# One v projection earlier in the hand-written order, held inverses, and elementwise work moved from GpSimd to VectorE and from VectorE to ScalarE

## The chip, the cores and the metric

One core of one Trainium2 chip runs the whole program. The metric is device microseconds (us) of one execution. An execution under the hardware profiler gives the trace that is read below; the other executions are timed without it.

## What is computed

The reference is one residual block over 2048 tokens of width 1024, in float32, with two causal token mixers side by side:

```
h = x @ w_in                          # split into q, k, v, z, b, a | q, k, v, z | gate_a, gate_b
A: q, k, v = silu(short causal conv of width 4); q, k normalized
   beta = sigmoid(b); g = -exp(a_log) * softplus(a + dt_bias)
   gated delta rule over 4 heads of 128: in a chunk a triangular system is inverted, a state S runs across chunks
   y_a = rmsnorm(o) * w * silu(z)
B: attention over a window of 128 tokens, 8 query heads, 2 key heads of 64, rotary on 16 of 64,
   a sink logit in the softmax's denominator; y_b = attention * silu(z)
merged = sigmoid(gate_a) * (y_a @ w_a) + sigmoid(gate_b) * (y_b @ w_b)
out = layernorm(2**0.25 * x + merged @ w_out) * ln_g + ln_b
```

## The kernel before, in words

The 2048 tokens go in four chunks of 512 (`NCH`). Every large product is made of three matmuls of a reduced-precision type (`prods`, L175 to L177): each operand is split into a high half and a low half (the rounding rest), and high x high, high x low and low x high are summed in PSUM. So a weight piece of 128 x 512 needs a copy that rounds (ScalarE, L156) and a subtraction that leaves the rest (GpSimd, L157). `split` does this the first time a piece is met, and stores both halves to DRAM (`keep`, L141); later chunks load the halves (L152). Most pieces are met in chunk 0, the output projection's at the start of chunk 1. Four buffers (`W_SPLIT`) hold pieces on their way.

**Order on TensorE.** It is written by hand. `ORDER` is a list of words, one per projection: `kv` (keys and values of B with b and a), `k0 q0 v0` (one head's k, q, v of A), `z0`, `w0` (a pair of query groups of B with their z), `g` (a gate), `p` (a quarter of the output projection of the chunk before). Chunk 0 has its own list, `ORDER_FIRST`. These dense pieces are cut into steps, and between steps the class `Order` puts the steps of side tasks: it counts planned nanoseconds, and a side task's next step is written when its due time (`LAT_...`) has passed. `finish` writes a task's steps out at once where something needs its end. TensorE executes in exactly the written order; on the other engines and on the DMA queue of SyncE (SP) a scheduler orders the instructions when the program is built, and each engine then executes its own list in order.

**The side tasks of a head of A.** `front` (L352) makes k's and q's statistics and products; the 32 x 32 diagonal blocks go through DRAM (L400, L402) into the tile `su`. `inverse` (L423) is spawned `LAT_M` = 4400 planned ns later and inverts them on VectorE: `small_inverse` (L918) begins with a memset into `su` (L924) that is pinned to its place in the written order, then pairs of a product and a reduction (L936, L937), sixteen of each, written at a pace of 420 + 40n ns. `levels` (L428) joins the blocks on TensorE; `back` (L475) transposes v (L485), scales it (`vt`, L491), and runs four blocks of a chain in which TensorE and VectorE take turns (L497, `bt` L499, L502, `wc` L504, L508, S L509). It ends with `osum`, an rsqrt and `dt` (L522), and `delta_gate` (L525) follows. `back` of head 0 waits for v0.

**`conv_silu` (L309)** serves q, k and v: ScalarE moves PSUM into `xs` (L313), VectorE copies three halo columns in (L314) and out (L319), one scaled copy on ScalarE (L316), three multiply-adds (L318), a tanh, a product (L321). One buffer `xs` serves all.

**`attend` (L574)**, spawned by `window_q`, goes over 4 blocks of tokens for each of two groups, 32 blocks in all. Per block: scores for two key heads v (L591, L592), then for each v on its own: two masked maxima (L599), `nm`, `es`, exponentials with a sum on ScalarE (L605, L608), sum plus sink, times 2, reciprocal, and the product with the 128 x 512 tile on VectorE (L614). `LAT_SM` = 9200 planned ns later TensorE transposes the first half's probabilities (L622), then the second's, and multiplies by the values (L630).

`project` (L674) and `layer_norm` (L703) finish the chunk before, at the start of the next one: four pieces `p`, then normalization on VectorE, which reads gamma and beta from DRAM (L716).

Of the kernel before, what the change touches and what calls it, by code (L numbers as in the profile page):

```python
# [8 lines left out]
F32 = mybir.dt.float32  # L9
F32R = mybir.dt.float32r  # L10
AF = mybir.ActivationFunctionType
# [5 lines left out]
P = 128  # L17
# [22 lines left out]
LAT_INV, LAT_B, LAT_S, LAT_N, LAT_SM, LAT_D, LAT_M, LAT_K, LAT_Q, LAT_Y, LAT_F, LAT_W = 29600, 2700, 2300, 7700, 9200, 5400, 4400, 1400, 7900, 8300, 4100, 2300  # L40
# [4 lines left out]
ORDER = "kv k0 q0 p p p p k1 v0 q1 g w0 v1 z0 k2 q2 v2 g g g k3 z1 g q3 g w1 v3 g g g g z2 g g g z3 g g g"  # L45
# [16 lines left out]
def build(tc, xt, xn, wk, wg, par, lnp, cst, out, seq=2048):  # L62
    nc = tc.nc
    NCH = seq // T
    with ExitStack() as ctx:
# [43 lines left out]
        nc.vector.tensor_scalar(nsink, sink, -1.0, None, ALU.mult)  # L109
        nea = const.tile([P, NH], F32, name="nea")  # L110
# [32 lines left out]
        def split(key, src, width=512, out=None):  # L143

            both = None if out else pw.tile([P, 2, 528], F32R, name="wb", bufs=W_SPLIT)[:, :, :width]
            hi, lo = out or (both[:, 0], both[:, 1])
            if key in kept_w:
                if out:
                    for n, w in enumerate(out):
                        nc.sync.dma_start(out=w.bitcast(F32), in_=kept_w[key][:, n])  # L150
                else:
                    nc.sync.dma_start(out=both.bitcast(F32), in_=kept_w[key])  # L152
                return hi, lo
            raw = pw.tile([P, 528], F32, name="w", bufs=W_RAW)[:, :width]
            nc.sync.dma_start(out=raw, in_=src)
            nc.scalar.activation(hi, raw, AF.Copy)  # L156
            nc.gpsimd.tensor_tensor(lo, raw, hi.bitcast(F32), ALU.subtract)  # L157
            keep(key, both)
            return hi, lo
# [59 lines left out]
        def start(c):  # L219
# [6 lines left out]
            for k in range(KT):  # L226
# [6 lines left out]
                if not k % 4:  # L233
                    wb = [pw.tile([P, 2, 528], F32R, name="wb", bufs=W_SPLIT)[:, :, :512] for _ in FIRST]
                    wh, wl = ([b[:, n] for b in wb] for n in range(2))
                    for i in range(3):
                        nc.vector.tensor_copy(wh[i], first[i + 3 * (k // 4)])
                        nc.gpsimd.tensor_tensor(wl[i], first[i + 3 * (k // 4)], wh[i].bitcast(F32), ALU.subtract)
                        keep((FIRST[i], k // 4), wb[i])
# [69 lines left out]
        def conv_silu(c, j, h, ps):  # L309
# [4 lines left out]
            nc.vector.tensor_copy(xs[:, :3], halo[:, n])  # L314
# [4 lines left out]
            nc.vector.tensor_copy(halo[:, n], xs[:, T:])  # L319
# [32 lines left out]
        def front(c, h):  # L352
# [32 lines left out]
            nc.gpsimd.tensor_tensor(qd, qd, q4, ALU.mult)  # L385
# [37 lines left out]
        def inverse(h, su, xi):  # L423
            yield from small_inverse(tc, pt.tile([P, 256], F32, name="xt"), su, xi.rearrange("p (c i) -> p c i", i=32))
            nc.sync.dma_start(out=at(scr_p[h % 2], 0, [[P, P], [1, P]]), in_=xi)
            yield None, 0
# [98 lines left out]
        def delta_gate(c, h, on):  # L525
# [12 lines left out]
            nc.gpsimd.tensor_tensor(c.yAl[:, h], y, c.yAh[:, h].bitcast(F32), ALU.subtract)  # L538
# [21 lines left out]
        def query_rows(c, b0, qr):  # L560
# [5 lines left out]
            lo = pa.tile([P, 2, 2, P], F32, name="pT").bitcast(F32R)  # L566
            for v, vs_ in enumerate(HALF):
                q = c.qT[v][:, b0:b0 + 2]
                nc.scalar.activation(q[vs_], pst[vs_], AF.Copy)
                nc.vector.tensor_tensor(lo[vs_], pst[vs_], q[vs_].bitcast(F32), ALU.subtract)  # L570
# [3 lines left out]
        def attend(c, gp):  # L574
# [8 lines left out]
            for b in range(NB):  # L583
                k0 = 0 if c.i or b else P
                nk = 256 - k0
# [7 lines left out]
                ss = []  # L593
                for v in range(2):
                    sk = slice(4 * v + 2 * gp, 4 * v + 2 * gp + 2)
                    s = pa.tile([P, 2, 256], F32, name="s")
                    mx = sm.tile([P, 2], F32, name="mx")
                    for g in range(2):
                        nc.vector.tensor_tensor_reduce(s[:, g, k0:], psc[v][:, g, k0:], band[:, k0:], 1.0, 2 * NEG,  # L599
                                                       ALU.add, ALU.max, mx[:, g:g + 1])  # L600
                    nm = sm.tile([P, 2], F32, name="nm")
                    nc.vector.scalar_tensor_tensor(nm, mx, -0.125, nsink[:, sk], ALU.mult, ALU.min)  # L602
                    es = sm.tile([P, 2], F32, name="es")
                    nc.vector.tensor_tensor(es, nm, sink[:, sk], ALU.add)
                    nc.scalar.activation(es, es, AF.Exp)  # L605
                    su = sm.tile([P, 2], F32, name="sum")
                    for g in range(2):
                        nc.scalar.activation(s[:, g, k0:], s[:, g, k0:], AF.Exp, bias=nm[:, g:g + 1], scale=0.125,  # L608
                                             accum_out=su[:, g:g + 1])
                    nc.vector.tensor_tensor(su, su, es, ALU.add)  # L610

                    nc.vector.tensor_scalar(su, su, 2.0, None, ALU.mult)
                    nc.vector.reciprocal(su, su)
                    nc.vector.tensor_tensor(s[:, :, k0:], s[:, :, k0:], su.unsqueeze(2).to_broadcast([P, 2, nk]), ALU.mult)  # L614
                    ss.append(s)
# [22 lines left out]
                nc.gpsimd.tensor_tensor(c.yBl[:, gs, bs], y, c.yBh[:, gs, bs].bitcast(F32), ALU.subtract)  # L638
# [279 lines left out]
def small_inverse(tc, t, su, xi):  # L918
# [5 lines left out]
    tc.keep_in_program_order(nc.vector.memset(view(su, 33, [[66, 16]]), 0.0))  # L924
# [7 lines left out]
    for i in range(30, -1, -2):  # L932
# [5 lines left out]
        yield None, 420 + 40 * n  # L938
# [74 lines left out]
```

## Time and profile before

| | us |
|---|---|
| three executions, median (lowest to highest) | 1702.67 (1699.82 to 1708.82) |
| the profiled execution | 1703.38 |
| its span, first to last instruction | 1701.6 |
| TensorE busy / VectorE / ScalarE / GpSimd | 1623.3 / 1019.1 / 534.6 / 313.1 |
| mean granted TensorE clock, share of full | 0.987 |

Engines are named PE (TensorE matmul), PEld (its weight loads), DVE (VectorE), ACT (ScalarE), POOL (GpSimd), SP (SyncE; SPq is its queue of DMA issues). L12 is line 12 of the kernel before. A row of a group of instructions reads: line, engine, operation, output tile<-input tiles, shape, count | busy us, mean ns of one | idle time of the engine just before them, and what ended it. A row of the waits reads: engine, tile and line that waited <- what it waited for: us in total, times, longest. A row of the timeline reads: start, duration, engine, line, operation, count, and in brackets the idle time before it and its releaser. A row of stages reads: from:to, length, busy us (and instructions) of each engine, granted clock, share of DMA time, GB/s.

### The profile page before, as it was taken

To read this page: it belongs to the slowest core of one execution; us is meant where nothing else is said; L and a number is where in the kernel's file an instruction comes from. 1 tells how busy PE (TensorE), PEld (TensorE's weight loads), DVE (VectorE), ACT (ScalarE), POOL (GpSimd) and SP (SyncE) were. 2 spreads that over 40 slices of the span, in tenths; PEclk is the share of its full clock that TensorE was granted. 3 is DMA by queue.
4 is the path that set the end of the run, shared out by engine and by line. 5 is a ranking of instruction groups with operands and counts; after the bars stand their busy time and mean duration, and the time that the engine had idled before them with its cause. 6 is when DMAs were issued, how large, how long until landed. Compare 5 with 4: busy or idle time off the path is not lost.

```text
span 1701.6 us, 27308 instructions
## 1 busy us (share of the span) xinstructions
PE 1623.3 (95%) x9846; PEld 1365.4 (80%) x9846; DVE 1019.1 (60%) x3202; ACT 534.6 (31%) x1484; POOL 313.1 (18%) x318
## 2 busy tenths in 40 slices
PE   8989999989979999999999999999999999999997
PEld 6867878878968778788987877888887887888787
DVE  6687678447577756434548774733556777463155
ACT  3454445424222432331302343323120244232110
POOL 4543544441401111010101111001010111100001
PEclk9999999999999999999999999999999999999999
DMA  8765676657765446457566644646566654564762
GB/s 304 237 228 186 200 256 200 232 194 251 249 240 177 141 127 177 141 161 238 170 213 208 184 138 129 192 137 199 170 195 212 201 159 119 149 190 143 272 207 77
DMA packets 189159, 323.39 MB, mean 190 GB/s; under 512 B 31072, under 2 KB 45408, under 8 KB 188896
## 3 DMA queue, kind: packets, MB, share of 16 engines
q1 hardware_dynamic: 185184, 316.40, 58.5%
q0 software_dynamic: 3840, 5.25, 1.5%
q8 instruction: 78, 1.28, 0.3%
q14 instruction: 57, 0.47, 0.1%
HBM read 244.97 MB, written 71.37 MB: 186 GB/s over the span
## 4 chain that ended last, share of the span: by engine, by line
PE 80%; DVE 9%; DMA 7%; ACT 1%; issue 1%; SPq 1%; POOL 1%; ACTq 0%; DVEq 0%; POOLq 0%
PE mm L175 22%; PE mm L177 21%; PE mm L176 21%; DMA wb<-kw_o 2%; PE pp L630 2%; PE pp L622 2%; DVE xt L936 1%; PE pp L591 1%; DVE xi L937 1%; PE pd L508 1%; PE pp L592 1%; PE pd L502 1%; DMA s<-in_lnp 1%; DVE k L318 1%; PE pd L510 1%
## 5 line engine op out<-in xcount | busy, mean ns | idle before, releaser
L175 PE MATMUL mm<-xh,wb 128*128 128x512 f32 x1128 | 472.0, 418 | 3.1 <-DVE mv L692 1.6
L177 PE MATMUL mm<-xh,wb 128*128 128x512 f32 x1128 | 447.4, 397 | 0.0
L176 PE MATMUL mm<-xl,wb 128*128 128x512 f32 x1128 | 445.8, 395 | 0.0
L177 PEld LDWEIGHTS mm<-xh,wb 128*128 128x128 f32 x1128 | 213.1, 189 | 50.3
L175 PEld LDWEIGHTS mm<-xh,wb 128*128 128x128 f32 x1128 | 214.1, 190 | 47.2 <-issue 4.5
L176 PEld LDWEIGHTS mm<-xl,wb 128*128 128x128 f32 x1128 | 215.0, 191 | 37.4
L157 POOL TENSOR_TENSOR wb<-w,wb 128x512 fp32r<-128x512 f32 (+1 forms) x110 | 146.3, 1332 | 182.2 <-ACT wb L156 167.8
L175 PE MATMUL mm<-wb,s 128*128 128x256 f32 x384 | 111.8, 291 | 10.3 <-DMA wb<-kw_o 6.3
L175 PE MATMUL mm<-wb,xh 128*128 128x256 f32 (+1 forms) x384 | 114.0, 297 | 6.6 <-DVE ba L264 3.2
L176 PE MATMUL mm<-wb,xh 128*128 128x256 f32 (+1 forms) x384 | 108.5, 282 | 0.3 <-POOL wb L157 0.3
L176 PE MATMUL mm<-wb,s 128*128 128x256 f32 x384 | 108.5, 283 | 0.0
L177 PE MATMUL mm<-wb,s 128*128 128x256 f32 x384 | 108.5, 283 | 0.0
L177 PE MATMUL mm<-wb,xl 128*128 128x256 f32 (+1 forms) x384 | 108.1, 281 | 0.0
L156 ACT ACTIVATE wb<-w 128x512 fp32r<-128x512 f32 (+1 forms) x110 | 68.9, 628 | 106.9 <-PE mm L177 54.6
L936 DVE TENSOR_TENSOR xt<-su,xi 128x16 f32<-128x16 f32 (+15 forms) x256 | 88.4, 345 | 5.7
L175 PEld LDWEIGHTS mm<-wb,s 128*128 128x128 f32 x384 | 73.1, 190 | 14.6 <-DMA wb<-kw_o 8.2
L608 ACT ACTIVATE s<-s,nm 128x256 f32<-128x256 f32 (+1 forms) x128 | 62.6, 491 | 68.4 <-DVE nm L602 68.4
L175 PEld LDWEIGHTS mm<-wb,xh 128*128 128x128 f32 x384 | 72.5, 189 | 10.0 <-issue 6.2
L937 DVE TENSOR_REDUCE xi<-xt 128x8 f32<-128x16 f32 (+15 forms) x256 | 74.7, 292 | 6.2
L176 PEld LDWEIGHTS mm<-wb,s 128*128 128x128 f32 x384 | 73.1, 190 | 0.2
L177 PEld LDWEIGHTS mm<-wb,s 128*128 128x128 f32 x384 | 73.0, 190 | 0.0
L176 PEld LDWEIGHTS mm<-wb,xh 128*128 128x128 f32 x384 | 72.4, 189 | 0.7 <-POOL wb L157 0.6
(664 smaller groups left out, 3104.5 us busy)
## 6 DMA issues: line engine op xcount, KB each, us to landing
wb<-kw_h SPq DMA_DIRECT2D x96, 512.0 KB, 4.1
wb<-kw_g SPq DMA_DIRECT2D x96, 512.0 KB, 4.0
w<-in_wg SPq DMA_DIRECT2D x106, 256.0 KB, 4.1
wb<-kw_b SPq DMA_DIRECT2D x48, 512.0 KB, 4.2
wb<-kw_o SPq DMA_DIRECT2D x36, 512.0 KB, 5.0
kw_h<-wb SPq DMA_DIRECT2D x32, 512.0 KB, 3.6
kw_g<-wb SPq DMA_DIRECT2D x32, 512.0 KB, 3.5
wb<-kw_q SPq DMA_DIRECT2D x24, 512.0 KB, 3.9
```

The source lines that it names most:

```text
L156: nc.scalar.activation(hi, raw, AF.Copy)
L157: nc.gpsimd.tensor_tensor(lo, raw, hi.bitcast(F32), ALU.subtract)
L175: nc.tensor.matmul(ps, sh, mh, start=(first and i == 0), stop=False)
L176: nc.tensor.matmul(ps, sh, ml, start=False, stop=False)
L177: nc.tensor.matmul(ps, sl, mh, start=False, stop=(last and i == n))
L318: nc.vector.scalar_tensor_tensor(r, xs[:, s:s + T], convw[:, n, s:s + 1], r, ALU.mult, ALU.add)
L502: nc.tensor.matmul(ps, q_[:, b], bt, start=True, stop=True)
L608: nc.scalar.activation(s[:, g, k0:], s[:, g, k0:], AF.Exp, bias=nm[:, g:g + 1], scale=0.125, accum_out=su[:, g:g + 1])
L622: nc.tensor.transpose(psp[:, kb, g], ss[v][:, g, P * kb:P * kb + P], ident)
L630: nc.tensor.matmul(psY[64 * v:64 * v + 64], c.vs[b + kb][:, 64 * v:64 * v + 64], pTs[v][:, kb], start=(kb == kbs[0]), stop=(kb == 1))
L936: nc.vector.tensor_tensor(tx[:, :, :, :n], u, x, ALU.mult)
L937: nc.vector.tensor_reduce(xi[:, :, i:i + 2], tx[:, :, :, :n], AX.X, ALU.add)
```

## The change

- In `ORDER` (chunks 1 to 3) `v0` stands after the first `p`, where it stood after `k1`.
- `LAT_M` goes from 4400 to 10000. The memset into `su` leaves `small_inverse` and is issued in `inverse`, after the VectorE instruction that was written last before it; it is no longer pinned. The pace of the sixteen steps is 300 + 35n.
- Subtractions and a product on GpSimd go to VectorE: L157, L238, L385, L538, L638.
- The halo copies L314 and L319 go to ScalarE.
- `query_rows`: the low half is made of the whole 128 x 512 tile at once (one copy on ScalarE, one subtraction on VectorE) instead of two subtractions of 64 partitions.
- `attend`: the small steps of the two key heads are joined into tiles of four columns, the sink's exponential carries a factor 2, and the product by the reciprocal becomes four scaled copies on ScalarE.

```diff
-LAT_M = 4400
+LAT_M = 10000
-ORDER = "kv k0 q0 p p p p k1 v0 q1 g w0 v1 z0 ..."
+ORDER = "kv k0 q0 p v0 p p p k1 q1 g w0 v1 z0 ..."
...
+        sink2 = const.tile([P, 8], F32, name="sink2")
+        nc.vector.tensor_scalar(sink2, sink, float(np.log(2.0)), None, ALU.add)
...
             nc.scalar.activation(hi, raw, AF.Copy)
-            nc.gpsimd.tensor_tensor(lo, raw, hi.bitcast(F32), ALU.subtract)
+            nc.vector.tensor_tensor(lo, raw, hi.bitcast(F32), ALU.subtract)
...
-            nc.vector.tensor_copy(xs[:, :3], halo[:, n])
+            nc.scalar.activation(xs[:, :3], halo[:, n], AF.Copy)
...
-            nc.vector.tensor_copy(halo[:, n], xs[:, T:])
+            nc.scalar.activation(halo[:, n], xs[:, T:], AF.Copy)
...
-            nc.gpsimd.tensor_tensor(qd, qd, q4, ALU.mult)
+            nc.vector.tensor_tensor(qd, qd, q4, ALU.mult)
...
         def inverse(h, su, xi):
+            with tc.issue_after(next(i for i in reversed(nc.cur_bb.bb.instructions) if i.engine == mybir.EngineType.DVE)):
+                nc.vector.memset(view(su, 33, [[66, 16]]), 0.0)
             yield from small_inverse(...)
...
-            nc.gpsimd.tensor_tensor(c.yAl[:, h], y, c.yAh[:, h].bitcast(F32), ALU.subtract)
+            nc.vector.tensor_tensor(c.yAl[:, h], y, c.yAh[:, h].bitcast(F32), ALU.subtract)
...
             lo = pa.tile([P, 2, 2, P], F32, name="pT").bitcast(F32R)
+            nc.scalar.activation(lo, pst, AF.Copy)
+            nc.vector.tensor_tensor(lo, pst, lo.bitcast(F32), ALU.subtract)
             for v, vs_ in enumerate(HALF):
                 q = c.qT[v][:, b0:b0 + 2]
                 nc.scalar.activation(q[vs_], pst[vs_], AF.Copy)
-                nc.vector.tensor_tensor(lo[vs_], pst[vs_], q[vs_].bitcast(F32), ALU.subtract)
                 nc.gpsimd.dma_start(out=q[HALF[1 - v]], in_=lo[vs_])
...
+                mx, nm, es, su = (sm.tile([P, 2, 2], F32, name=n) for n in ("mx", "nm", "es", "sum"))
+                for v, g in each:
+                    nc.vector.tensor_tensor_reduce(ss[v][:, g, k0:], psc[v][:, g, k0:], band[:, k0:], ..., mx[:, v, g:g + 1])
+                nc.vector.scalar_tensor_tensor(nm, mx, -0.125, heads(nsink), ALU.mult, ALU.min)
+                nc.vector.tensor_tensor(es, nm, heads(sink2), ALU.add)
+                for v, g in each:
+                    nc.scalar.activation(ss[v][:, g, k0:], ss[v][:, g, k0:], AF.Exp, bias=nm[:, v, g:g + 1], ..., accum_out=su[:, v, g:g + 1])
+                nc.scalar.activation(es, es, AF.Exp)
+                nc.vector.scalar_tensor_tensor(su, su, 2.0, es, ALU.mult, ALU.add)
+                nc.vector.reciprocal(su, su)
+                for v, g in each:
+                    nc.scalar.activation(ss[v][:, g, k0:], ss[v][:, g, k0:], AF.Copy, scale=su[:, v, g:g + 1])
...
-                nc.gpsimd.tensor_tensor(c.yBl[:, gs, bs], y, c.yBh[:, gs, bs].bitcast(F32), ALU.subtract)
+                nc.vector.tensor_tensor(c.yBl[:, gs, bs], y, c.yBh[:, gs, bs].bitcast(F32), ALU.subtract)
...
 def small_inverse(tc, t, su, xi):
-    tc.keep_in_program_order(nc.vector.memset(view(su, 33, [[66, 16]]), 0.0))
...
-        yield None, 420 + 40 * n
+        yield None, 300 + 35 * n
```

## Rows read from the trace of the kernel before

**Rows 1.** The page, busy time of each engine (share of the span), instructions.
```profile
PE 1623.3 (95%) x9846; PEld 1365.4 (80%) x9846; DVE 1019.1 (60%) x3202; ACT 534.6 (31%) x1484; POOL 313.1 (18%) x318
```

**Rows 2.** The waits of TensorE over the whole span.
```profile
PE pd L485 <- DVE v L321: 14.2, 3, 7.2
PE mm L175 <- DMA wb<-kw_o: 6.3, 10, 1.5
PE pd L502 <- DVE bt L499: 5.8, 4, 1.6
PE pp L591 <- DVE yb L635: 5.6, 1, 5.6
PE pd L534 <- DVE dt L522: 4.3, 1, 4.3
PE mm L175 <- DVE yBh L688: 3.9, 2, 3.4
PE pp L622 <- DVE x__2836 L452: 3.3, 1, 3.3
...
PE mm L176 <- POOL wb L157: 0.3, 1, 0.3
```

**Rows 3.** Stages of 25 us around two of the three waits for v; the clock stands before the DMA share.
```profile
500.00:525.00 25.00, 21.03 (x150) 19.72 (x151) 14.86 (x45) 7.68 (x25) 2.30 (x2) 0.86 0.41 146
...
1325.00:1350.00 25.00, 21.43 (x132) 19.09 (x131) 18.67 (x54) 7.92 (x25) 2.31 (x2) 0.86 0.52 173
```

**Rows 4.** The timeline of VectorE ahead of the first wait for v.
```profile
495.48 0.49 DVE L718 SCALAR_TENSOR_TENSOR yBh<-yBh,mv,s 128x256 f32<-128x256 f32 x1 [1.94 <-DMA s<-in_lnp]
...
503.14 0.69 DVE L321 SCALAR_TENSOR_TENSOR v<-xs,v 128x512 f32<-128x512 f32 x1
```

**Rows 5.** The timeline of VectorE at the longest stall for `su`.
```profile
446.88 0.07 DVE L924 MEMSET su<- 128x16 f32 x1 [5.95 <-DMA su<-scrm]
...
447.79 0.68 DVE L688 SCALAR_TENSOR_TENSOR yBh<-s,mm 128x512 f32<-128x512 f32 x1
```

**Rows 6.** The stage of chunk 0 after its start, busy us of each engine.
```profile
25.00:390.00 365.00, 344.32 (x1998) 283.86 (x1998) 245.71 (x718) 161.63 (x428) 158.84 (x137) 0.98 0.68 219
```

**Rows 7.** Groups of GpSimd in that stage.
```profile
L157 POOL TENSOR_TENSOR wb<-w,wb 128x512 fp32r<-128x512 f32 (+1 forms) x93 | 124.2, 1337 | 151.1 <-ACT wb L156 136.9 <-DMA w<-in_wg 4.3 <-PE pd L378 3.8
```

**Rows 8.** Groups of VectorE in that stage.
```profile
L318 DVE SCALAR_TENSOR_TENSOR k<-xs,par,k 128x512 f32<-128x512 f32 x12 | 13.2, 1100 | 1.9 <-ACT k L316 1.8
```

**Rows 9.** The same group in the stage from 800 to 1215 us.
```profile
L318 DVE SCALAR_TENSOR_TENSOR k<-xs,par,k 128x512 f32<-128x512 f32 x12 | 9.0, 747 | 0.3
```

**Rows 10.** Groups of VectorE over the whole span.
```profile
L614 DVE TENSOR_TENSOR s<-s,sum 128x512 f32<-128x512 f32 (+1 forms) x64 | 47.9, 757 | 0.6
...
L314 DVE COPY xs<-halo 128x3 f32<-128x3 f32 x48 | 14.7, 306 | 0.8
...
L612 DVE TENSOR_SCALAR sum<-sum 128x2 f32<-128x2 f32 x64 | 10.9, 182 | 0.7
...
L670 DVE TENSOR_TENSOR s<-vt,s 128x512 fp32r<-128x512 f32 x32 | 22.3, 698 | 8.0 <-ACT s L668 7.7
```

**Rows 11.** Groups of ScalarE over the whole span.
```profile
L608 ACT ACTIVATE s<-s,nm 128x256 f32<-128x256 f32 (+1 forms) x128 | 62.6, 491 | 68.4 <-DVE nm L602 68.4
...
L608 ACT ACTIVATION_READ_ACCUMULATOR s<-s,nm 128x1 f32 x128 | 24.0, 187 | 0.0
```

**Rows 12.** The timeline of TensorE, last score and first transpose of two softmax blocks.
```profile
605.23 0.28 PE L592 MATMUL pp<-kTl,qT 128*128 128x256 f32 x1
...
611.43 0.63 PE L622 MATMUL pp<-ct,s 128*128 128x128 f32 x4 [0.85 <-DVE osum L518]
...
1568.32 0.28 PE L592 MATMUL pp<-kTl,qT 128*128 128x256 f32 x1
...
1579.28 0.60 PE L622 MATMUL pp<-ct,s 128*128 128x128 f32 x4
```

**Rows 13.** The timeline of VectorE in the second of these blocks, the product by the reciprocal.
```profile
1572.88 0.68 DVE L614 TENSOR_TENSOR s<-s,sum 128x512 f32<-128x512 f32 x1
```

More of the change, by code (lines that the diff above doesn't have):

```diff
@@ L38 @@
 PE_R, PE_F, PE_T, PE_Q = 216, 218, 109, 45
-LAT_INV, LAT_B, LAT_S, LAT_N, LAT_SM, LAT_D, LAT_M, LAT_K, LAT_Q, LAT_Y, LAT_F, LAT_W = 29600, 2700, 2300, 7700, 9200, 5400, 4400, 1400, 7900, 8300, 4100, 2300
+LAT_INV, LAT_B, LAT_S, LAT_N, LAT_SM, LAT_D, LAT_M, LAT_K, LAT_Q, LAT_Y, LAT_F, LAT_W = 29600, 2700, 2300, 7700, 9200, 5400, 10000, 1400, 7900, 8300, 4100, 2300
 FIRST = ("h01", "h00", "h02")
 ORDER_FIRST = "start g kv w0 g k1 g g q1 g g g z0 v1 g z1 k2 q2 v2 w1 k3 g q3 g v3 g g g g z2 z3 g g"
-ORDER = "kv k0 q0 p p p p k1 v0 q1 g w0 v1 z0 k2 q2 v2 g g g k3 z1 g q3 g w1 v3 g g g g z2 g g g z3 g g g"
+ORDER = "kv k0 q0 p v0 p p p k1 q1 g w0 v1 z0 k2 q2 v2 g g g k3 z1 g q3 g w1 v3 g g g g z2 g g g z3 g g g"
 P_ALOG, P_DTB, P_DNW, P_SINK, P_CONV = 0, 4, 8, 9, 17
@@ L237, in start @@
                         nc.vector.tensor_copy(wh[i], first[i + 3 * (k // 4)])
-                        nc.gpsimd.tensor_tensor(wl[i], first[i + 3 * (k // 4)], wh[i].bitcast(F32), ALU.subtract)
+                        nc.vector.tensor_tensor(wl[i], first[i + 3 * (k // 4)], wh[i].bitcast(F32), ALU.subtract)
                         keep((FIRST[i], k // 4), wb[i])
@@ L584, in attend @@
                 k0 = 0 if c.i or b else P
-                nk = 256 - k0
                 kbs = [1] if k0 else [0, 1]
@@ L592, in attend @@
                         nc.tensor.matmul(psc[v][:, g, k0:], c.qT[v][:, b, g], kT[2 + v][:, ks], start=False, stop=True)
[L593 to L615, printed above, removed]
@@ new lines, in attend @@
+                heads = lambda a: a.rearrange("p (v g) -> p v g", v=2)[:, :, 2 * gp:2 * gp + 2]
+                mx, nm, es, su = (sm.tile([P, 2, 2], F32, name=n) for n in ("mx", "nm", "es", "sum"))
+                ss = [pa.tile([P, 2, 256], F32, name="s") for _ in range(2)]
+                each = [(v, g) for v in range(2) for g in range(2)]
+                for v, g in each:
+                    nc.vector.tensor_tensor_reduce(ss[v][:, g, k0:], psc[v][:, g, k0:], band[:, k0:], 1.0, 2 * NEG,
+                                                   ALU.add, ALU.max, mx[:, v, g:g + 1])
@@ new lines, in attend @@
+                nc.vector.scalar_tensor_tensor(nm, mx, -0.125, heads(nsink), ALU.mult, ALU.min)
+                nc.vector.tensor_tensor(es, nm, heads(sink2), ALU.add)
+                for v, g in each:
+                    nc.scalar.activation(ss[v][:, g, k0:], ss[v][:, g, k0:], AF.Exp, bias=nm[:, v, g:g + 1], scale=0.125,
+                                         accum_out=su[:, v, g:g + 1])
+                nc.scalar.activation(es, es, AF.Exp)
+                nc.vector.scalar_tensor_tensor(su, su, 2.0, es, ALU.mult, ALU.add)
```

## The prediction

> **What bounds the kernel now.** I read the busy shares first: TensorE is busy in 95% of the span, no other engine in more than 60% [rows 1]. Its products are not touched by the change, so what can be won is what TensorE waits, and what it loses in the slower stretches that follow long waits. The waits of TensorE come next [rows 2]. The largest is 14.2 us in 3 waits, one in each of chunks 1 to 3: the transposes of v wait for the last multiply of v's convolution. Then come weights of the output projection (6.3), `bt` (5.8), the output of a softmax block (5.6, once), `dt` at the end of chunk 0 (4.3, once), the eviction of an output projection (3.9) and a copy in `levels` (3.3, once). The stages around the v waits show the second price: the granted clock is 0.86 over 25 us [rows 3]; as its two levels are 2.4 and 1.2 GHz, that is (1 - 0.86) x 2 x 25 = 7.0 us at 1.2 GHz, partly spent waiting, the rest at half rate.
>
> Why v is late is seen on VectorE: its last multiply ends at 503.8, and the queue holds the layer norm of the chunk before, which itself sits 1.9 us for gamma and beta from DRAM [rows 4]. The eviction wait has another origin: VectorE stands 5.95 us before the pinned memset into `su`, because `su` is still on its way, and the eviction L688 that TensorE needs comes behind it [rows 5].
>
> **The change, part by part.** The sum starts from the profiled execution, 1703.4 us (span 1701.6), 0.7 above the median of the runs.
>
> *v0 forward.* It issues two 512 KB loads on SP, 24 matmuls, three operations on ScalarE besides the tanh, and four large ones on VectorE, all now ahead of three output projections and their loads. v is then made before the layer norm is spawned, so its 14.2 us of waits go [rows 2], and about 5 us of half-rate work with them: the two stages shown hold 14 us at 1.2 GHz [rows 3], of which roughly 7 lie behind the waits, worth 3.5, and I give the third wait 1.5. That is 19.2. What is late next is `vt` and `bt`, which stand in the same VectorE queue behind the same layer norm and the same stall [rows 4]. Between nothing and all of the 14.2 may come back there; I take 1.5 us a chunk, 4.5, near the stall of 1.9, since the hand-written order leaves two steps between v's transposes and the first use of `bt`. Net -14.7. On SP, a projection takes all four weight buffers, so one projection straight behind another waits for its loads; with v0 between the first two, one of three such joins in a chunk goes. 6.3 us in 10 waits [rows 2]: I take -1.5, between -6.3 and +3 (the projections' loads are the same ones, only later).
>
> *Inverses held.* The memset loses its pin, so the 5.95 us stall and the eviction behind it go [rows 5]: of the 3.9 us of waits for evictions, 3.4 in the longest [rows 2], and about 1 us at half rate; -4.5, between 0 and -5. The price: an inverse is written 5600 planned ns later and runs some 3300 faster (16 steps, the n's sum to 272: 16 x 120 + 5 x 272), so `levels` comes about 2 us later. In the middle of a chunk this is hidden by the dense pieces; it shows where the chain of `back` is already bare: at the end of chunk 0 (`dt`, 4.3) and once per later chunk (the 1.6 us waits for `bt`) [rows 2]. I take +2 and 3 x 0.7, together +4, between 0 and 2 us in each of four places, 8.
>
> *GpSimd's work on VectorE.* In the stage of chunk 0, VectorE is busy 245.7 of 365 us [rows 6]. 93 subtractions come to it [rows 7]; on VectorE such an operation takes 0.698 [rows 10], so +65, and 9 more for the other three lines in this stage. Off it go about a quarter of the 47.9 us of L614 in the span, of the 14.7 of L314 and of the 10.9 of L612 with steps like it: some 30. And operations that ran beside GpSimd get shorter: L318 takes 1100 ns here and 747 in a later stage, where GpSimd does little [rows 8, 9]; for the 36 such operations of the stage alone that is about 10 us, and I take 25 for all. 245.7 + 74 - 30 - 25 = 265, or 73% against 67%: not a new bound. What it does to TensorE: the 3.3 us for the copy in `levels` sat behind three stretched multiplies of this kind, so I take it off with 1.5 of half rate, -4.8. The 5.6 us for the softmax output is as likely kept as not, since its queue gets subtractions in place of the stretching: -3.6, half of 5.6 + 1.5. Against this, each subtraction waits for ScalarE's rounding and that for a load, and behind it on VectorE stand evictions and softmax steps; the stores to DRAM on SP wait for it, and behind those stand loads. No row prices this. From below it is 0 (TensorE waited 0.3 us in all for GpSimd's low halves [rows 2]), from above 0.35 us on each of 93 pieces, 33 us; I take +4, near the lower end, because the subtraction itself gets 0.64 us shorter [rows 7, 10].
>
> *Softmax.* The first half's factor now waits for four exponentials instead of two: 2 x (0.49 + 0.19), of which about 0.1 overlaps [rows 11], and scaling two tiles on ScalarE takes 0.98 against 0.68 on VectorE, less the joined small steps: +1.2. In the ordinary block the product ends at 1573.6 and the transposes start at 1579.3 [rows 12, 13], 5.7 us to spare; nothing there. Three blocks, one in each later chunk, have their transposes 6.2 us after the last score instead of 11.0, and wait already [rows 12]: 3 x 1.2 = +3.6, between 0 and 3 x 2.5. The halo copies now stand on ScalarE between operations of the same convolution, and the single subtraction in `query_rows` replaces two; both are hidden by the matmuls of the next pieces, and without that cover would cost under 0.3 us apiece (L314 takes 306 ns [rows 10]).
>
> The Trainium skill ("ScalarE: Activation LUTs", section on rules for kernel authors) says that multiplications belong on VectorE. By it the four scaled copies are a step back; the row agrees, 128 x 0.49 = 63 us on ScalarE for 47.9 on VectorE, and the sum would be right only as long as that chain has room, which is one of the rivals.
>
> Sum: -14.7 - 1.5 - 4.5 + 4 - 4.8 - 3.6 + 4 + 3.6 = -17.5. 1703.4 - 17.5 - 0.7 = **1685 us**, forecast as 1674 to 1694.
>
> **The rivals.** *The wait moves on* (chance 0.17): v is ready, but `vt` sits behind the layer norm's stall and `bt` waits instead. For: the stall of 1.9 us stays in the queue [rows 4]. Against: two steps of dense work stand between. Then 14 of the 19.2 us stay, 1685 + 10 = 1695 to 1700, no change.
> *Scaled copies bind* (0.05): ScalarE's longer chain uses up the room in chunk 0's eight blocks too, at 1.2 us each, 1685 + 10 = 1695. Against it stands the 5.7 us of room [rows 12, 13], although that block is of chunk 3. This is where the rule of that page of the Trainium skill would lead.
> *VectorE's waits vanish altogether* (0.17): no softmax wait, no `bt` waits, no new ones. Without the +4.5, +4, +4, +3.6 and with the other half of the softmax wait (3.6), 1685 - 20 = 1665.
> *Late low halves* (0.11), the one that is slower: in chunk 0, VectorE takes the 93 subtractions in a queue with softmax, convolutions and inverses, and TensorE waits for the low half of a piece. Price: the mean lateness times 93. It decides above (17.5 + 4 + 8.5) / 93 = 0.32 us apiece; at 0.4 us it gives 1685 + 33 = 1718. For: one engine then does all of it, at 73% [rows 6]. Against: 0.3 us of such waits with GpSimd, whose subtraction takes 1.34 us [rows 2, 7].
>
> **How the numbers follow.** The forecast has 0.50, the rivals 0.17, 0.05, 0.17 and 0.11. About 0.5% (8.5 us) is what a measurement of this kernel can tell from no change: faster is below 1694, slower above 1711. Faster: 0.50 + 0.17 = 0.67; slower 0.11; same, the rest, 0.22. The range runs from the third rival's 1665, with a few us for the clock, to the first one's 1700, with the upper bound of the softmax term (3.9): 1661 to 1703. It leaves out the slower rival and the far side of the others.
>
> **What would show it.** Right: no wait of L485 for v; no stall of VectorE at the memset; L318 at about 750 ns in chunk 0; GpSimd busy under 100 us; VectorE 70 to 75% busy from 25 to 390 us; transposes of the three tight blocks later by some 1.2 us. Wrong: `bt` waits of 3 us or more at the place where v's were; TensorE waiting for `wb` from VectorE line 157 by more than 10 us in chunk 0; waits of L622 for the scaled tile in ordinary blocks; new waits for `kw_o` loads.

## The result, and the profile after

| us | before | after |
|---|---|---|
| median of 8 executions each (lowest to highest) | 1701.97 (1698.84 to 1708.82) | 1714.89 (1711.18 to 1717.95) |
| the profiled execution, and its span | 1703.38, 1701.6 | 1713.42, 1711.7 |

The ratio after to before is 1.0073, with an interval of 1.0055 to 1.0091: slower by 12 us, where 17.5 us less was forecast. The page of the changed kernel, its busy line (to be held against [rows 1]):

```profile
PE 1629.8 (95%) x9846; PEld 1372.3 (80%) x9846; DVE 984.3 (58%) x3015; ACT 600.7 (35%) x1692; POOL 88.9 (5%) x138
```

The work moved as the change says: GpSimd fell from 313.1 to 88.9 us, and VectorE did not grow. The waits of TensorE over the span tell where the time went. (L177 is a dense product, L455 the first product of `levels`, L623 the transposes in `attend`; lines are those of the changed kernel.)

```profile
PE mm L177 <- DVE rope L886: 9.3, 3, 3.3
PE pd L455 <- DMA p__2747<-scrp: 8.1, 1, 8.1
PE mm L177 <- DMA wb<-kw_o: 7.5, 8, 2.3
PE pp L623 <- ACT s L616: 6.4, 3, 2.1
PE pd L455 <- DMA p__1876<-scrp: 6.3, 1, 6.3
...
PE pd L507 <- DVE bt L504: 4.1, 5, 2.0
...
PE pd L455 <- DMA p__5181<-scrp: 2.4, 1, 2.4
```

Against [rows 2], the 14.2 us for v, the 5.6 for the softmax output and the 3.3 for the copy in `levels` are gone. New are 16.8 us in three waits of `levels` for `p`, the block of the inverse that comes back from DRAM, and 9.3 us in three waits for `rope`, one in each of chunks 0, 2 and 3. TensorE's idle time, its span less its busy time, grew by 3.6 us (78.3 to 81.9), its busy time for the same 9846 products by 6.5. The stages of the changed kernel, with the columns of [rows 3], show the clock:

```profile
25.00:390.00 365.00, 338.98 (x1971) 281.50 (x1970) 240.71 (x727) 175.19 (x476) 17.98 (x28) 0.96 0.66 217
...
925.00:950.00 25.00, 20.48 (x127) 18.94 (x127) 14.58 (x50) 5.35 (x18) 1.08 (x2) 0.86 0.66 203
1340.00:1365.00 25.00, 20.30 (x140) 19.10 (x139) 16.03 (x53) 6.31 (x19) 2.10 (x3) 0.86 0.63 203
```

In chunk 0 the granted clock fell from 0.98 [rows 6] to 0.96: (1 - 0.96) x 2 x 365 = 29 us at the lower of its two levels against 15 before; the clock is given to hundredths, so each figure is good to some 4 us. The two stages of 25 us have 0.86, the very figure of the v stages [rows 3]; only now they lie where TensorE waits for `rope`.

The start of each chunk, read from the timeline of TensorE as the first 264-column product of the key and value projection, puts the loss in place:

| us | start | chunk 0 | chunk 1 | chunk 2 |
|---|---|---|---|---|
| before | 32.4 | 358.3 | 421.4 | 412.3 |
| after | 32.2 | 364.8 | 416.7 | 418.4 |

Chunk 0 lost 6.5 us and chunk 2 6.1, chunk 1 gained 4.7, and chunk 3 with the end of the span lost 2.4 (477.2 to 479.6).

**Chunk 0.** `v0` is not moved there, and still it lost 6.5 us. This is head 2 of chunk 0 in the timeline, the engines' rows put together: the product k k^T (L391), the inverse's memset (L428) and last step (L937), the store of its result and the load of `p` on SP, and the first product of `levels`.

```profile
203.59 0.38 PE L391 MATMUL pd<-k 128*128 128x128 f32 x2
...
220.98 0.07 DVE L428 MEMSET su<- 128x16 f32 x1
...
244.62 0.42 DVE L937 TENSOR_REDUCE xi<-xt 128x8 f32<-128x256 f32 x1
...
245.53 0.95 SPq L430 DMA_DIRECT2D scrp<-xi  x1
...
249.34 1.75 SPq L443 DMA_DIRECT2D p__2747<-scrp  x4
...
250.97 0.31 PE L455 MATMUL pd<-p__2747,m 32*32 32x32 f32 x2 [8.11 <-DMA p__2747<-scrp]
```

And the same points of the kernel before:

```profile
203.40 0.27 PE L389 MATMUL pd<-k 128*128 128x128 f32 x1
...
214.09 0.07 DVE L924 MEMSET su<- 128x16 f32 x1 [0.95 <-DMA su<-scrm]
...
237.99 0.41 DVE L937 TENSOR_REDUCE xi<-xt 128x8 f32<-128x256 f32 x1
...
242.27 0.24 PE L450 MATMUL pd<-p__2776,m 32*32 32x32 f32 x2
```

Counted from k k^T, the inverse now starts at +17.4 for +10.7 and ends at +41.4 for +35.0. `levels` has its place in TensorE's order at about +39 in both (250.97 - 8.11 - 203.59 = 39.3; 38.9 before), so TensorE stands. Of the 8.1 us some 6.4 are the late end; about 2 more come from the way over DRAM, 5.9 us from the end of the inverse to the product (245.04 to 250.97), where 3.9 were room enough before (238.40 to 242.27). For head 1 the end went from +33.1 to +41.4, and the wait is 6.3. Heads 0 and 3 wait for nothing: head 0 even ended earlier, at +33.7 for +36.9, so planned nanoseconds of delay are not microseconds of the trace.

**Chunks 2 and 3.** In the timeline of VectorE ahead of the `rope` wait of chunk 2, the layer norm of the chunk before (L719, L720) now fills the queue; the last row is TensorE's:

```profile
925.25 0.88 DVE L719 SCALAR_TENSOR_TENSOR yBh<-yBh,mv,s 128x256 f32<-128x256 f32 x2 [0.54 <-DMA s<-in_lnp]
...
930.15 0.88 DVE L720 SCALAR_TENSOR_TENSOR yBl<-yBl,rs,s 128x256 f32<-128x256 f32 x2
...
931.93 0.22 DVE L886 TENSOR_TENSOR rope<-mm,ct 128x64 f32<-128x64 f32 x1
...
932.30 0.36 PE L177 MATMUL mm<-wb,xh 128*128 128x256 f32 x1 [3.26 <-DVE rope L886]
```

It is the burst that v waited behind before [rows 4]; it starts after the fourth output projection, which `v0` has pushed back by one piece.

### The profile page after: what moved, and what is told of

It reads as the page before. It is cut to its first block, busy times and chain, and to the rows that moved or that the text cites. A ratio compares the mean times of both kernels' runs of the same rounds, so it can differ in the third digit from the quotient of the medians.

```text
span 1711.7 us, 26967 instructions
## 1 busy us (share of the span) xinstructions
PE 1629.8 (95%) x9846; PEld 1372.3 (80%) x9846; DVE 984.3 (58%) x3015; ACT 600.7 (35%) x1692; POOL 88.9 (5%) x138
## 3 DMA queue, kind: packets, MB, share of 16 engines
q8 instruction: 78, 1.28, 0.3%
## 4 chain that ended last, share of the span: by engine, by line
PE 80%; DMA 9%; DVE 6%; issue 1%; ACT 1%; SPq 1%; POOL 0%; DVEq 0%; ACTq 0%; POOLq 0%
PE mm L177 22%; PE mm L179 21%; PE mm L178 21%; DMA wb<-kw_o 2%; PE pp L631 2%; PE pp L623 2%; DMA s<-in_lnp 1%; PE pd L513 1%; PE pp L596 1%; PE pp L597 1%; DMA scrm<-m 1%; DMA wb<-kw_kv 1%; PE pd L507 1%; PE pd L515 1%; PE pd L502 1%
## 5 line engine op out<-in xcount | busy, mean ns | idle before, releaser
L177 PE MATMUL mm<-xh,wb 128*128 128x512 f32 x1128 | 473.7, 420 | 0.8 <-DMA wb<-kw_h 0.8
L177 PEld LDWEIGHTS mm<-xh,wb 128*128 128x128 f32 x1128 | 215.2, 191 | 46.2 <-issue 6.2
L177 PE MATMUL mm<-wb,xh 128*128 128x256 f32 (+1 forms) x384 | 116.7, 304 | 11.6 <-DVE rope L886 9.3
L177 PE MATMUL mm<-wb,s 128*128 128x256 f32 x384 | 110.4, 288 | 9.8 <-DMA wb<-kw_o 7.5
L178 PE MATMUL mm<-wb,xh 128*128 128x256 f32 (+1 forms) x384 | 110.7, 288 | 0.0
L159 DVE TENSOR_TENSOR wb<-w,wb 128x512 fp32r<-128x512 f32 (+1 forms) x110 | 75.5, 688 | 44.2 <-ACT wb L158 40.1
L177 PEld LDWEIGHTS mm<-wb,xh 128*128 128x128 f32 x384 | 75.1, 196 | 14.9 <-issue 12.6
L177 PEld LDWEIGHTS mm<-wb,s 128*128 128x128 f32 x384 | 72.4, 188 | 13.7 <-DMA wb<-kw_o 9.4
L936 DVE TENSOR_TENSOR xt<-su,xi 128x16 f32<-128x16 f32 (+15 forms) x256 | 76.4, 299 | 5.5
L937 DVE TENSOR_REDUCE xi<-xt 128x8 f32<-128x16 f32 (+15 forms) x256 | 74.7, 292 | 5.2
L178 PEld LDWEIGHTS mm<-wb,xh 128*128 128x128 f32 x384 | 75.1, 196 | 0.2
L179 PEld LDWEIGHTS mm<-wb,xl 128*128 128x128 f32 x384 | 74.9, 195 | 0.0
L178 PEld LDWEIGHTS mm<-wb,s 128*128 128x128 f32 x384 | 72.3, 188 | 0.5 <-DVE wb L159 0.3
```

Of the source, the lines that this page charges most:

```text
L159: nc.vector.tensor_tensor(lo, raw, hi.bitcast(F32), ALU.subtract)
L177: nc.tensor.matmul(ps, sh, mh, start=(first and i == 0), stop=False)
L178: nc.tensor.matmul(ps, sh, ml, start=False, stop=False)
L179: nc.tensor.matmul(ps, sl, mh, start=False, stop=(last and i == n))
L936: nc.vector.tensor_tensor(tx[:, :, :, :n], u, x, ALU.mult)
L937: nc.vector.tensor_reduce(xi[:, :, i:i + 2], tx[:, :, :, :n], AX.X, ALU.add)
```

## The experiments

Each ratio is to runs of the kernel before on the same chip, with its interval; 0.001 is 1.7 us. The runs were on three chips, so runs are held against each other by their ratios. From the two traces there were three theories of the loss: A, the longer delay makes the inverses end behind the place of `levels`; B, it is VectorE's added subtractions that make them late; C, v's new place only moves its waits onto other work. Against C stood D, that v's new place gains by itself and the loss lies elsewhere.

**The delay undone.** `LAT_M` back at 4400, the rest of the change kept.

```diff
-LAT_M = 10000
+LAT_M = 4400
```

> The changed kernel with LAT_M back at 4400; the memset stays unpinned and the pace stays new. Theory A (the hold makes the inverses late): the memset comes again 11 to 13 us after the product k k instead of 14 to 17, TensorE's waits of the levels for p (17.8 us in three heads) fall under 3 us, with the half-rate stretches behind them 15 to 25 us go: about 1695 us. Theory B (the subtractions crowd VectorE in chunk 0): the inverses of chunk 0 stay as long (24 to 25 us), half or more of those waits stays, 1707 to 1715 us.

Measured: 1697.83 us, ratio 0.9974 (0.9960 to 0.9988), so 0.0099 or 17 us below the change, as A has it; of the 16.8 us between the two traced spans 11.4 are TensorE's idle time (81.9 to 70.5) and 5.4 its busy time. Head 2 of chunk 0, the same points in its timeline:

```profile
194.63 0.38 PE L391 MATMUL pd<-k 128*128 128x128 f32 x2
...
204.73 0.07 DVE L428 MEMSET su<- 128x16 f32 x1
...
227.58 0.42 DVE L937 TENSOR_REDUCE xi<-xt 128x8 f32<-128x256 f32 x1
...
233.96 0.24 PE L455 MATMUL pd<-p__2733,m 32*32 32x32 f32 x2 [1.28 <-DMA p__2733<-scrp]
```

Start +10.1, end +33.4, and a wait of 1.28 in place of 8.11. Chunk 0 took 348.0 us against 364.8. What did not go, against A, is a wait for `p` in chunk 1, which grew from 2.4, and the waits for `kw_o` grew:

```profile
PE mm L177 <- DMA wb<-kw_o: 9.2, 9, 3.1
...
PE pd L455 <- DMA p__5137<-scrp: 6.2, 1, 6.2
```

**The subtraction of the weight pieces back on GpSimd**, the rest of the change kept.

```diff
-            nc.vector.tensor_tensor(lo, raw, hi.bitcast(F32), ALU.subtract)
+            nc.gpsimd.tensor_tensor(lo, raw, hi.bitcast(F32), ALU.subtract)
```

> The changed kernel with one line back on GpSimd: the subtraction that makes the low half of a weight piece (110 of them). Theory B (the subtractions crowd VectorE): the two longest inverses of chunk 0 shrink from 25 and 24 us to 21 and the levels' waits in chunk 0 (15.9 us) go, 1697 us. Theory A (the hold): VectorE gets slower beside GpSimd again, the inverses stay over 22 us, 8 us or more of those waits stays, 1710 to 1722 us.

Measured: 1725.83 us, ratio 1.0123 (1.0101 to 1.0145), 0.005 above the change, and a little above A's range. So this part gains some 8.5 us, and B falls: the waits for `p` of heads 1 and 2 stay at 3.5 and 6.9 us without it. The groups of this kernel, GpSimd over the span and VectorE in chunk 0, show both prices near those of [rows 7, 8]; the last row is the same VectorE group in the changed kernel:

```profile
L159 POOL TENSOR_TENSOR wb<-w,wb 128x512 fp32r<-128x512 f32 (+1 forms) x110 | 146.3, 1333 | 251.9 <-ACT wb L158 233.7 <-DMA w<-in_wg 9.8 <-DMA kw_g<-wb 3.3
...
L320 DVE SCALAR_TENSOR_TENSOR k<-xs,par,k 128x512 f32<-128x512 f32 x12 | 12.2, 1014 | 7.8 <-ACT k L318 7.7
...
L320 DVE SCALAR_TENSOR_TENSOR k<-xs,par,k 128x512 f32<-128x512 f32 x12 | 9.0, 747 | 0.1
```

**v back**, the rest of the change kept.

```diff
-ORDER = "kv k0 q0 p v0 p p p k1 q1 g ..."
+ORDER = "kv k0 q0 p p p p k1 v0 q1 g ..."
```

> The changed kernel with v0 after k1 again in chunks 1 to 3. Theory C (the layer norm's burst on VectorE delays what stands behind it, v or the rotary step of w0, so that moving v only moves the wait): the waits of 3.3 and 3.0 us for the rotary step in chunks 2 and 3 go, waits for v of about 14 us come back, and the time changes by under 8 us either way. Rival D (v forward gave its full 19 us and the losses are elsewhere): 1730 us or more.

Measured: 1706.28 us, ratio 1.0020 (1.0008 to 1.0032), 0.0053 or 9 us below the change, just more than C allowed, although its waits show v's return (4.5 more stand under `nci`, at the same transposes):

```profile
PE pd L490 <- DVE v L323: 6.7, 2, 4.3
```

The `rope` waits of chunks 2 and 3 are gone, as C has it. With smaller waits that went, TensorE's idle time is 7.3 us less than in the change (81.9 to 74.6), of 8.2 in the traced spans.

**v forward alone**, in the kernel before: the same edit of `ORDER` and nothing else.

> The kernel before with v0 forward alone. Theory C: the waits for v (14.2 us) go, waits of about 3 us each for the rotary step of w0 and for the head's m2 appear in two or three chunks, with the half rate behind them: 1692 to 1700 us. Rival D: only bt waits of under 2 us a chunk replace them, 1684 us or less.

Measured: 1714.39 us, ratio 1.0072 (1.0054 to 1.0089). By itself it costs as much as the whole change, and D falls. C had the kind of the new waits, but not the time: it is 14 us above C's range. Its waits:

```profile
PE pd L389 <- DVE yBh L719: 5.3, 2, 3.2
...
PE mm L175 <- DVE rsq L873: 3.3, 1, 3.3
PE pd L450 <- DMA p__10226<-scrp: 3.3, 1, 3.3
```

v's 14.2 us are gone; k k^T (L389) now waits for the layer norm (L719), a dense piece for its `rsq`, and `levels` for an inverse that started behind it (in chunk 2 at +20.9 from k k^T, +11.6 before). In the traced spans 3.0 of 8.8 us are idle time of TensorE, the rest its busy time, so the price is not in the waits alone.

**Both undone**: v back and the delay at 4400, the other parts kept. This kernel is the base of those that follow.

> The changed kernel with v of head 0 back behind k1 and the inverses' delay back at 4400; all other parts of the change stay. If the two losses are separate and add up (17.1 from the delay, 8.6 from v): 1714.9 - 17.1 - 8.6 = 1689 us, with the waits for v back at 11 to 14 us and the levels waiting for p under 4 us in all. If both undo the same waits (the levels' for p), it gives 1696 to 1700 us, no better than the delay alone undone (1697.8).

Measured: 1695.66 us, ratio 0.9940 (0.9920 to 0.9960). Most of both gains is there, 0.0133 of 0.0099 + 0.0053. As ratios the two cases are 0.992 and 0.9965 or more; it lies between, nearer the first, and the interval reaches the first and almost the second. The waits for v are 15.4 us again, and the softmax blocks (L623) wait almost nothing:

```profile
PE pd L490 <- DVE v L323: 15.4, 3, 6.4
...
PE pp L623 <- ACT s L616: 0.7, 1, 0.7
```

Two parts lose, then, and the rest of the change gains 10 us.

**The softmax as it was**, on that base.

```diff
-                heads = ...   (joined steps, four scaled copies on ScalarE)
+                for v in range(2):   (the steps for each key head, the product on VectorE)
```

> The kernel of the run before (v back, delay 4400), and the softmax as it was: each head group apart, the row product on VectorE. If the new softmax costs what its tight blocks show (2.13 us of wait against 0.85 in three of them, and half clock behind them), this is 4 to 8 us faster than the run before it. If the joined steps and the product's move help elsewhere by freeing VectorE (some 20 us of it per chunk), it is 2 to 6 us slower.

Measured: 1705.34 us, ratio 1.0004 (0.9988 to 1.0019): the new softmax gains 0.0064, 11 us, where a cost was expected. The edit undoes the joined steps and the scaled copies together, so what each is worth stays open. Rows of VectorE's groups and of TensorE's waits in this kernel; the first is ScalarE's copies in the base:

```profile
L616 ACT ACTIVATE s<-s,sum 128x256 f32<-128x256 f32 x120 | 51.0, 498 | 2.2 <-DVE sum L614 2.1
...
L621 DVE TENSOR_TENSOR s<-s,sum 128x512 f32<-128x512 f32 x60 | 40.1, 687 | 0.4
...
PE pd L455 <- DMA p__5231<-scrp: 3.4, 1, 3.4
...
PE pd L455 <- DMA p__3498<-scrp: 2.2, 1, 2.2
PE pd L455 <- DMA p__1904<-scrp: 2.2, 1, 2.2
```

VectorE has 40 us of products again (1039.4 us busy in all, 990.0 in the base), and the waits for `p` are longer than the base's 2.5, 1.6 and under 0.6. The profiled executions differ by 2.6 us only, so these rows carry a part of the 11; the rest is not shown.

**The delay alone**, in the kernel before: 10000, the free memset, the new pace.

> The kernel before with the inverse part of the change alone: delay 10000, the memset free to go ahead, the new pace of the inverse's steps. If the delay costs by itself what undoing it gave (17.1 us), 1702 + 12 to 18 = 1714 to 1720 us, with the memsets at +15 us or later behind kk and the levels waiting for p by 8 us or more. If it costs only beside the forward v and the work moved to VectorE, it is within 4 us of before (1698 to 1706 us).

Measured: 1728.23 us, ratio 1.0139 (1.0115 to 1.0163), 24 us, more than either theory had. Its waits show the two heads of chunk 0, and the tight softmax blocks (L625) beside them:

```profile
PE pd L453 <- DMA p__2790<-scrp: 8.7, 1, 8.7
PE pp L625 <- DVE s L617: 7.4, 4, 2.4
...
PE pd L453 <- DMA p__1910<-scrp: 4.2, 1, 4.2
```

**v one place earlier only**, on the base: behind the four output projections, ahead of `k1`.

```diff
-ORDER = "kv k0 q0 p p p p k1 v0 q1 g ..."
+ORDER = "kv k0 q0 p p p p v0 k1 q1 g ..."
```

> The kernel of the first run (v back, delay 4400) with v0 ahead of k1 and behind the four output pieces: p p p p v0 k1 q1. The layer norm's start is not moved by this. If the loss of the forward v comes from the layer norm being put a piece later, this takes the waits for v (11 to 14 us, a third of it in each of three chunks) down to under 3 us at no other wait, and is 6 to 12 us faster than the first run. If the loss comes from v's own convolution standing ahead of kk and the decay's work on VectorE, the waits move there, and it is within 4 us of the first run.

Measured: 1688.84 us, ratio 0.9898 (0.9877 to 0.9920), 7 us below the base, with intervals that meet at 0.9920. The gain is as in the first case, its mechanism is not: the wait passed from v (15.4) to k, and only shrank.

```profile
PE pd L367 <- DVE k L323: 11.6, 3, 5.3
```

**The layer norm late, v where it was**, on the base.

```diff
-ORDER = "kv k0 q0 p p p p k1 v0 q1 g ..."
+ORDER = "kv k0 q0 p p p k1 p v0 q1 g ..."
```

> The kernel of the run with v back and delay 4400 (1695.7 us, ratio to before 0.994), with the last output piece moved behind k1: p p p k1 p v0 q1. v keeps its place; the layer norm, which starts behind the fourth output piece, comes one piece (some 5.5 us) later, and k1 one earlier. If the late layer norm is what the forward v costs, this is 5 to 10 us slower (ratio 0.997 to 1.000), with new waits for rope, m or the inverses' p right behind the layer norm. If the layer norm's place costs nothing, it is the same or up to 4 us faster (0.992 to 0.994), since k1's convolution also starts earlier.

Measured: 1682.39 us, ratio 0.9874 (0.9851 to 0.9898), 11 us faster than the base. The theory that a late layer norm is by itself what costs falls. Its waits:

```profile
PE pd L507 <- DVE bt L504: 13.9, 8, 3.0
...
PE pd L391 <- DVE yBl L720: 3.7, 3, 1.8
PE pd L490 <- DVE rs L875: 3.3, 3, 1.6
```

The convolution of k1 runs before the layer norm here, v's among its steps, and what is late is spread over waits of 3 us and less, most of them for `bt`. The rows shown do not explain the gain: `bt` (5.3 in the base), `yBl` and `rs` are 15.6 us more, as much as the waits for v that went. Yet TensorE's idle time is 8.0 us less (69.7 to 61.7) and its busy time 4.5, since many small waits shrank; why they did was not tested.

**Three smaller parts undone, each on the base.** The memset pinned at the head of the inverse, with the old pace:

> The kernel with v back and delay 4400 (ratio 0.994), with the memset of su in its old place at the head of the inverse and the inverse's old pace. If the free memset takes the 5.95 us wait of the kernel before out of VectorE's order and that is worth something, this is 3 to 6 us slower. If the wait was beside other waits, it is within 2 us. If the new pace (300 + 35 n for 420 + 40 n) packs the inverse too tightly among the other work, this is 2 to 6 us faster.

Measured: 1693.99 us, ratio 0.9932 (0.9909 to 0.9955): no difference from the two together. The small work back on GpSimd (L240, L387, L543, L639):

> The kernel with v back and delay 4400 (ratio 0.994), with the other pieces of GpSimd's work put back there: the product with q in decays, the low halves of yA and yB, and the first weights' low halves; the weight pieces' subtraction stays on VectorE. The waits for yb and x come back (8.9 us in the kernel before). If that is all, it is 4 to 9 us slower (0.9965 to 0.9995). If VectorE's freed time (some 5% of its work) is worth as much, it is within 2 us; if GpSimd, now nearly empty, is quick enough for these, and VectorE is the late one, 3 to 6 us faster.

Measured: 1699.05 us, ratio 0.9970 (0.9953 to 0.9987), 5 us slower, with intervals that overlap a little; the wait for yb did not come back (1.6 us, 1.3 in the base). The halo copies and the q rows' halves on VectorE:

> The kernel with v back and delay 4400 (ratio 0.994), with the halo copies and the q rows' halves on VectorE as before. ScalarE loses some 60 us, VectorE gains two short copies a convolution. If VectorE's queue is what the late inverses and v come from, this is 3 to 8 us slower (0.996 to 0.999). If those copies lie in VectorE's free time, it is within 2 us. If the copies on ScalarE delay the convolution's first step, and with it v (15.4 us of waits in three chunks), it is 2 to 6 us faster.

Measured: 1691.53 us, ratio 0.9935 (0.9912 to 0.9959): no difference. (ScalarE's busy time fell by 18 us, not by 60.)

**v ahead of the last output projection**, on the base, to tell v's place from the layer norm's.

```diff
-ORDER = "kv k0 q0 p p p p k1 v0 q1 g ..."
+ORDER = "kv k0 q0 p p p v0 p k1 q1 g ..."
```

> The kernel of the run with v back and delay 4400 (ratio to before 0.994), with v0 one place further on in the change's own direction: p p p v0 p k1 q1, ahead of the last output piece only. The layer norm comes one piece later, as in the change and as in the run with p p p k1 p v0 (0.9874). If what the change's v costs is its place early among the output pieces (behind the first one, in the stretch where the inverse of head 0 runs), this is as good as that run: 0.986 to 0.991, and the levels of chunk 1's first head wait under 2 us. If v ahead of k1 is what costs, since k1 and q1 are then behind the layer norm and kk waits, it is 0.994 to 0.999, with L391 waiting 3 us in each of three chunks as with the change's order and delay 4400 (0.9974).

Measured: 1685.35 us, ratio 0.9879 (0.9856 to 0.9901). With the first run of all (0.9974) as its counterpart, two places of v are worth 16 us. Its trace is of its fastest execution, 1677.54 us. Its waits, against 9.2 for `kw_o` and 6.2 for `p` there:

```profile
PE pd L391 <- DVE wc L509: 8.8, 3, 3.3
...
PE mm L177 <- DMA wb<-kw_o: 3.5, 6, 1.0
```

No wait for `p` of chunk 1 is left among those of 0.3 us or more. L391 waits its 3 us in each of three chunks, as the second case had it, and it is less than the 15.4 us for v that it replaces.

**The delay at 7000**, on the base.

> The kernel with v back and the delay at 7000, between 4400 (0.994) and 10000 (1.002). If the loss grows with the delay in proportion, 0.9977, give or take 0.002. If it is a matter of passing the levels' written place, as the waits of two heads in chunk 0 show, most of it comes late and this is 0.993 to 0.996.

Measured: 1720.37 us, ratio 1.0100 (1.0077 to 1.0123), 27 us above the base and worse than 10000 with the same order (1.0020). Both cases missed. Head 1 of chunk 0:

```profile
126.16 0.38 PE L391 MATMUL pd<-k 128*128 128x128 f32 x2
...
141.24 0.07 DVE L428 MEMSET su<- 128x16 f32 x1
...
164.94 0.41 DVE L937 TENSOR_REDUCE xi<-xt 128x8 f32<-128x256 f32 x1
...
170.49 0.31 PE L455 MATMUL pd<-p__1868,m 32*32 32x32 f32 x2 [6.32 <-DMA p__1868<-scrp]
```

In the base the same inverse runs from +12.4 to +31.3, here from +15.1 to +39.2: 2.7 us later at its start, 7.9 at its end. The later inverse meets more of the next convolution (three multiplies of v and their product between its steps, two multiplies there), which is 1.4 us of the 5.2 by which it got longer. At 7000 `levels` waits for `p` in seven heads, 18.6 us together, at 10000 with the same order in three that count, 15.8. Why the shorter delay is the worse one stays open.

**The delay at 2400**, on the kernel with `p p p k1 p v0 q1`.

> The kernel with p p p k1 p v0 q1 and delay 4400 (0.9874), with the delay at 2400. If an earlier inverse is always better, the last waits of the levels for p (1.3, 1.6 and 0.8 us in three heads) go and it is 0.983 to 0.987. If 4400 is where the hold of VectorE begins, since the memset then stands in the queue ahead of su's arrival (5.95 us of such a wait in the kernel before), it is 0.989 to 0.995 with waits of VectorE for su.

Measured: 1700.24 us, ratio 0.9981 (0.9966 to 0.9997), 0.0107 above its own base, outside both ranges, and nearer the second. The memsets come no earlier (+13.4, +11.9, +10.2 us in the first heads, +13.6, +11.7, +10.1 at 4400), so the store and load of `su` set the start; VectorE stands 1.8 and 2.3 us for it in heads 1 and 2. What grew is in the waits:

```profile
PE mm L177 <- DMA wb<-kw_o: 7.0, 5, 3.0
```

`kw_o` was 2.6 there. The traces do not settle why the output weights are late.

**That order alone**, `p p p k1 p v0 q1` in the kernel before.

> The kernel before with one edit: the order p p p k1 p v0 q1. If this order is what v needs by itself (the waits for v, 14.2 us, go and the layer norm's delay hits nothing), it is 0.991 to 0.994. If it gains only beside the work that has left GpSimd and the joined softmax, it is within 0.996 to 1.002; v forward to the place of the change gave 1.0072 in this kernel.

Measured: 1703.13 us, ratio 0.9996 (0.9982 to 1.0010): no gain. The order pays only with the other parts of the change.

## Why the prediction was wrong

**v forward** was put at -14.7, with 1.5 us a chunk coming back. It is +9 us in the change, +12 alone. What v no longer waits for was right. The step that failed is what is late next: I looked for it at `vt` and `bt`, the next users of v, but the queue of VectorE does not belong to v. The burst behind which v had waited met `rope` in the change, and with v moved alone k k^T and the start of an inverse, work that the edit does not touch; in the change the half-rate stages came with it (0.86 before, 0.86 after). The place has a second price, which -1.5 for the `kw_o` joins had with the wrong sign: with v between the first two output projections and the delay at 4400 the waits for `kw_o` are 9.2 us, and `levels` waits 6.2 for one `p` of chunk 1; ahead of the last one they are 3.5 and nothing. In the first of these two runs that inverse ends 3.0 us later (+40.3 from k k^T, +37.3 in the other), and its way over DRAM to the product takes 9.8 us, 6.2 at most in the other. The idea was good, its distance was not: v one or two places earlier, or k1 one, gains 7 to 11 us on the base; k1's move alone, in the kernel before, gains nothing. "The wait moves on" was the nearest rival, but it named `bt`, which did not grow (5.8 us before, 4.1 after), and it could only eat the gain, not make a loss.

**The inverses held** were put at -4.5 + 4. They cost 17 us in the change, 14 with v back (1.0020 against 0.9940), 24 alone. The gain was not there: the pinned memset put back, with the old pace, makes no difference, and VectorE still stands 4.02 us for `su` in the changed kernel:

```profile
451.63 0.07 DVE L428 MEMSET su<- 128x16 f32 x1 [4.02 <-DMA su<-scrm]
```

The cost failed in two steps. "About 2 us later" took the faster pace as time won; but the steps of chunk 0 are spaced by what else VectorE does, and the inverses of heads 1 and 2 took 25.1 and 24.1 us (21.3 and 24.3 before), so a start later by 4.5 and 6.7 us became an end later by 8.3 and 6.4. And "hidden by the dense pieces in the middle of a chunk" was not measured against the room there. The timeline of before had it: 3.9 us from the end of head 2's inverse to `levels` (238.40 to 242.27), in which store and load must fit. I looked for bare places among the existing waits, where a slack that is nearly used up does not show.

**GpSimd's work on VectorE** was put at -4.4, with up to 33 us of late low halves as the slower rival. The rival falls: TensorE waits 0.3 us in all for a half of L159, and putting the subtraction back costs 8.5 us, the small pieces perhaps 5 more. L320 takes 747 ns in chunk 0, as forecast; with the subtraction on GpSimd it is 1014. The Trainium skill ("GPSIMD Engine Reference", specifications) says that GpSimd shares its SBUF interface with VectorE's instructions that have two SBUF inputs; these rows agree.

**Softmax** was put at +3.6. The rows seemed to agree, 6.4 us for the three tight blocks against 2.6; but of two runs that differ in the delay alone the one with 10000 has 6.4, the one with 4400 0.7 us in all. It was the held inverse. The part itself gains 11 us: the term had the wrong sign, as it priced only the chain inside a tight block. The rule of the Trainium skill ("ScalarE: Activation LUTs", rules for kernel authors), multiplications on VectorE, agrees with these rows on the price (51.0 us busy for the base's 120 copies, 40.1 for the 60 products of twice the size), and the time did not follow the price. That this is because VectorE has the late queue while ScalarE is busy 35% is likely but not shown, as the joined steps were undone in the same run.

The parts do not add up: +9 + 17 - 8.5 - 5 - 11 is about 2 us, where the change is +12. Each was taken against another base, so they need not add up; what one part frees another may fill, but no run shows which.

## What to carry to other kernels

When an edit removes a wait behind a burst on an in-order engine, follow the burst, not the data: list whatever will stand behind it next. When work is issued later, measure the slack of its consumer in the trace (end of the work, its store and load, the consumer's place), and take a pace in the plan as time only where the engine is free to keep it. Try a hand-set delay or place at values on both sides; here, of 2400 (with one order), 7000 and 10000 (with another) and 4400 (with both), only 4400 was good, and the loss did not grow in proportion to the distance from it.

## What the runs showed of the hardware that was not expected

TensorE's price of late work is more than the wait. Undoing the delay took 16.8 us from the traced span, but only 11.4 of them were idle time of TensorE; 5.4 were busy time for the same 9846 products (1629.8 to 1624.4 us), while the granted clock in chunk 0 rose from 0.96 to 0.98. Between its two levels, 2.4 and 1.2 GHz, (1 - clock) x 2 x 365 puts 29 and 15 us of chunk 0 at the lower one, some of it spent waiting. With v moved alone the busy time is even the larger part, 5.8 us of 8.8.

The best kernels measured, 0.9874 and 0.9879, keep the change's new softmax and its nearly empty GpSimd, and have the old delay and k1 one place or v two places earlier. That they come to the 1685 us forecast for the change is chance: the sum behind it had other terms.
